# Issuing the overflow path's weight copies from GpSimd's queue instead of ScalarE's

## The chip, the cores and the metric

The kernel runs on one core of a Trainium2 chip. The core has five engines, each with its own instruction stream: TensorE (PE in the profile; its weight loads are listed as PEld), VectorE (DVE), ScalarE (ACT), GpSimd (POOL) and SyncE (SP). A "q" behind an engine's name (SPq) means its sequencer: what it does there is waiting, branching or issuing a DMA, and it isn't counted as busy time. Engines tell each other of finished work by semaphores. The metric is device time in microseconds (us); lower is better.

## The reference, cut to what matters

The program is two transformer blocks on 256 tokens of width 1024. The first ends in a mixture of experts: a router picks one of 4 groups and two of its 8 experts for every token, and each expert is a small gated network (1024 to 2 x 256 to 1024). The reference sorts the 512 assignments by expert and runs every block of 128 slots:

```python
def run_block(args):
    xb, e, wb = args
    a = jax.nn.silu(xb @ w_gate[e]) * (xb @ w_up[e])
    return (a @ w_down[e]) * wb[:, None].astype(xb.dtype)
```

No expert may drop a token, however many it is given. The second block (three kinds of attention and a convolutional feed-forward network) reads the result.

## The kernel before, in words

The program runs mixer, mixture of experts (`moe`, L928) and second block (`block2`, L1294) one after the other. Instructions are written in Python; a scheduler sets the order on each engine, and a framework adds the semaphore waits.

**Experts.** `moe` gives each expert 32 slots and takes 4 experts at a time: 8 batches, loop over `b` at L1204. A batch needs 12 weight pieces of 1 MB (128 x 2048 f32): 8 for gate and up (`egu`), 4 for down (`edn`). For each piece `gateup1` (L1089) or `down` (L1148) does 4 products, which the trace shows as 8 matmuls. Between them come: the gather of tokens (L1072, copied to `xg` on L1074 and L1077), the gate (L1002 to L1004), two transposes (L1113, L1122), a copy of the down product out of PSUM to the tile `eo` (`out`, L1137, on ScalarE), and the scatter (L1131 on TensorE from `eo`, L1132 on VectorE into the residual `xT`).

**Weight loads.** `issue` (L280, its DMA is L284) sends the pieces from SyncE in the order in which they are used, into 23 buffers. The framework gives DMAs from SyncE and ScalarE eight semaphores in turn (DMAHW0 to DMAHW7), and a load waits until the load eight places before it has landed. There are 99 such loads; the last 13 of them stand behind the branch below.

**The two spare paths.** After batch 3 an extra set of 32 slots serves the expert with most tokens (`extra`). After batch 4 (`TURN + 1`), `overflow` (L1240) covers whatever doesn't fit even then. Each engine loads the largest remaining count (L1231) and branches (`tc.If`, L1247). Where the count is above 32, a loop over the batches (L1252) runs all tokens through all experts again, in pieces of 128 x 512 that the inner function `part` copies from HBM (L1255, L1256). Its tiles `wp` share the tag "eo" of pool `tm`, and so the two buffers of the `eo` tiles of L1137.

With these inputs the branch isn't taken: no instruction of L1248 to L1291 is in the trace. What remains of the path is the branch on every engine, with its code in the program, and a few instructions on the other arm of the branch, on which the framework moves the semaphores by as much as the skipped loop would have moved them, so that waits placed after the branch are the same on both ways. The loop's 48 copies a round, dealt over 8 semaphores, would add 6 x 16 = 96 to each.

Of the kernel before, what the change touches and what calls it, by code (L numbers as in the profile page):

```python
# [222 lines left out]
class Prog:  # L223
# [1016 lines left out]
    def overflow(self, tm, pm, psum, hn, W, pos, thr, most):  # L1240


        tc, nc, I = self.tc, self.nc, self.I
        v, a, te = nc.vector, nc.scalar, nc.tensor
        mm = te.matmul
        xT, g2 = self.xT, self.modc[:, 40:48]
        with tc.If(most > CAP, preferred_fallthrough_block=False):  # L1247
            Wo = pm.tile([P, 2, NE], F32, name="Wo")  # L1248
            v.tensor_tensor(out=Wo, in0=pos, in1=thr.unsqueeze(1).to_broadcast([P, 2, NE]), op=OP.is_gt)
            v.tensor_tensor(out=Wo, in0=Wo, in1=W, op=OP.mult)  # L1250
            Wo = Wo.rearrange("p q (b j) -> p q j b", j=4)
            with tc.For_i(0, NE // 4, 1) as b:  # L1252
                for j in range(4):
                    def part(name, i):
                        w = tm.tile([P, 512], F32, name="wp", tag="eo")  # L1255
                        a.dma_start(w, self.I[name].rearrange("b i p (j f) -> b j i p f", j=4)[bass.ds(b, 1), j, i]  # L1256
                                    .rearrange("o p f -> (o p) f"))
                        return w

                    gu = [psum("gu", 2) for _ in range(2)]  # L1260
                    for d in range(KD):
                        w = part("egu", d)
                        o = psum("x", 2)
                        for q in range(2):
                            te.transpose(o[:, q * P:(q + 1) * P], hn[:, q, d * P:(d + 1) * P], self.co("ident"))
                        hT = tm.tile([P, T], F32, name="hT", tag="ga")
                        a.activation(hT, o[:, :T], AF.Identity, scale=self.cols[:, 24 + d:25 + d], bias=self.modc[:, 24 + d:25 + d])
                        for q in range(2):
                            mm(gu[q], hT[:, q * P:(q + 1) * P], w, start=d == 0, stop=d == KD - 1)
                    aT = [tm.tile([P, 2, P], F32, name=n, tag=n, bufs=1) for n in ("aT", "PT")]  # L1270
                    for q in range(2):
                        th = tm.tile([P, 512], F32, name="th", tag="eo")[:, 0:256]
                        ac = tm.tile([P, 256], F32, name="ga", tag="ga")
                        a.activation(th, gu[q][:, 0:256], AF.Tanh, scale=0.5)
                        v.scalar_tensor_tensor(out=ac, in0=th, scalar=1.0, in1=gu[q][:, 0:256], op0=OP.add, op1=OP.mult)
                        v.scalar_tensor_tensor(out=ac, in0=ac, scalar=Wo[:, q, j, bass.ds(b, 1)], in1=gu[q][:, 256:512],
                                               op0=OP.mult, op1=OP.mult)
                        o = psum("x", 2)
                        for k in range(2):
                            te.transpose(o[:, k * P:(k + 1) * P], ac[:, k * P:(k + 1) * P], self.co("ident"))  # L1280
                        a.copy(aT[q], o[:, 0:256].rearrange("p (k s) -> p k s", k=2))
                    for nh in range(2):
                        wd = [part("edn", 2 * nh + k) for k in range(2)]
                        for q in range(2):
                            for i in range(4):
                                d = 4 * nh + i
                                o = psum("c", 2)
                                for k in range(2):
                                    mm(o[:, :P], wd[k][:, i * P:(i + 1) * P], aT[q][:, k], start=k == 0, stop=k == 1)
                                v.scalar_tensor_tensor(out=xT[:, d, q * P:(q + 1) * P], in0=o[:, :P], scalar=g2[:, d:d + 1],  # L1290
                                                       in1=xT[:, d, q * P:(q + 1) * P], op0=OP.mult, op1=OP.add)  # L1291
# [534 lines left out]
```

## Time and profile before

| | us |
|---|---|
| median of 3 runs | 1007.67 (1006.49 to 1008.81) |
| the profiled execution's own time | 1006.2 |
| its span, first to last instruction | 1004.4 |
| TensorE busy in the span | 928.5 |
| batches 0 to 7 of the experts, about | 341 to 553 |
| the branch, by engine | 342 (POOL), 463 (ACT), 467 (PE), 468 (DVE), 486 to 506 (SP) |

The last two lines are positions in the span. The weight loads are read in three ways: the order in which SyncE issues them (the timeline of SP), how long one takes from issue to landing (the DMA list of a stretch with one issue in it), and what the DMA engines move (the windows: "DMA share" 1.0 means that all 16 are busy).

### The profile page before, as it was taken

How to read it: one execution, taken by the hardware profiler on the slowest of the kernel's cores; microseconds unless marked ns; L12 is line 12 of the kernel's file. 1: busy time of each engine (PE TensorE's matmuls, PEld its weight loads, DVE VectorE, ACT ScalarE, POOL GpSimd, SP SyncE). 2: the span in 40 equal slices, each digit the busy share in tenths (PEclk: the TensorE clock that was granted, in tenths of full speed). 3: DMA queues.
4: the chain of work that ended last, by engine and by line, in shares of the span. 5: the costliest groups of instructions: out<-in, count | busy, mean ns of one | idle time of the engine just before them, and what ended most of it. 6: DMA issues, size and time to landing. Idle time of an engine off the chain costs nothing. (4 is left out here: it accounts for less than half of the span.)

```text
span 1004.4 us, 17784 instructions
## 1 busy us (share of the span) xinstructions
PE 928.5 (92%) x6870; PEld 761.9 (76%) x6870; DVE 604.9 (60%) x1463; ACT 473.3 (47%) x1006; POOL 13.0 (1%) x28
## 2 busy tenths in 40 slices
PE   4899899999999899997698999899998999999995
PEld 2678888999999545443232898788898889999994
DVE  2468699664663524223123884787769687676764
ACT  3546866555443122121112765476754565555553
POOL 0000000000000000000000000000001000000001
PEclk9899899999999799998989999999999999999998
DMA  8977367669558599999989654643245344555501
GB/s 358 408 275 283 123 243 264 248 233 421 223 204 355 196 420 416 413 422 418 418 344 421 250 189 149 250 152 137 92 169 189 126 169 168 193 185 174 205 1 43
DMA packets 37387, 249.76 MB, mean 249 GB/s; under 512 B 4272, under 2 KB 5040, under 8 KB 8368
## 3 DMA queue, kind: packets, MB, share of 16 engines
q1 hardware_dynamic: 37008, 248.01, 64.0%
q8 instruction: 56, 0.92, 0.4%
q10 hardware_dynamic: 288, 0.55, 0.2%
q14 instruction: 35, 0.29, 0.1%
HBM read 247.49 MB, written 1.05 MB: 247 GB/s over the span
## 5 line engine op out<-in xcount | busy, mean ns | idle before, releaser
L301 DVE TENSOR_TENSOR wlo<-w,whi 128x512 fp32r<-128x512 f32 (+2 forms) x426 | 287.9, 683 | 152.8 <-ACT whi L300 137.5
L300 ACT CAST whi<-w 128x512 fp32r<-128x512 f32 (+2 forms) x426 | 257.7, 611 | 253.1 <-PE ps_a L317 195.2
L316 PE MATMUL ps_a<-hh,whi 128*128 128x256 f32 x304 | 79.1, 292 | 4.9 <-ACT hh L612 3.1
L317 PE MATMUL ps_a<-hl,whi 128*128 128x256 f32 x304 | 78.5, 289 | 0.0
L1132 DVE SCALAR_TENSOR_TENSOR xT<-ps_c,modc,xT 128x256 f32<-128x256 f32 x72 | 33.1, 483 | 72.7 <-PE ps_c L1131 72.6
L316 PE MATMUL ps_a<-h4h,whi 128*128 128x256 f32 x304 | 76.1, 283 | 0.2 <-ACT h4h L343 0.2
L317 PE MATMUL ps_a<-h4l,whi 128*128 128x256 f32 x304 | 76.1, 283 | 0.0
L1089 PE MATMUL ps_gu<-w,xg 128*32 128x512 f32 x512 | 68.7, 618 | 6.5 <-issue 6.5
L316 PEld LDWEIGHTS ps_a<-hh,whi 128*128 128x128 f32 x304 | 59.4, 196 | 9.1 <-ACT hh L612 3.3
L316 PE MATMUL ps_a<-h2h,whi 128*128 128x256 f32 x248 | 64.2, 289 | 0.5 <-DVE kn L1509 0.5
L317 PE MATMUL ps_a<-h2l,whi 128*128 128x256 f32 x248 | 63.0, 284 | 0.0
L317 PEld LDWEIGHTS ps_a<-hl,whi 128*128 128x128 f32 x304 | 59.6, 196 | 2.0 <-issue 1.2
L316 PEld LDWEIGHTS ps_a<-h4h,whi 128*128 128x128 f32 x304 | 58.1, 192 | 1.2 <-ACT h4h L343 0.6
L317 PEld LDWEIGHTS ps_a<-h4l,whi 128*128 128x128 f32 x304 | 58.2, 192 | 0.3
L1131 PE MATMUL ps_c<-PT,eo 128*128 128x256 f32 (+1 forms) x144 | 41.9, 410 | 13.1 <-ACT eo L1137 12.1
L1131 PEld LDWEIGHTS ps_c<-PT,eo 128*128 128x128 f32 (+1 forms) x144 | 24.3, 192 | 37.3 <-ACT eo L1137 16.4
L1072 PEld LDWEIGHTS ps_x<-Ph,hn 128*128 128x128 f32 x256 | 34.0, 198 | 22.4 <-issue 17.6
L321 PE MATMUL ps_a<-hh,wlo 128*128 128x256 f32 x304 | 49.9, 288 | 0.3 <-DVE wlo L301 0.3
L316 PEld LDWEIGHTS ps_a<-h2h,whi 128*128 128x128 f32 x248 | 47.4, 191 | 2.9 <-issue 1.8
L321 PE MATMUL ps_a<-h4h,wlo 128*128 128x256 f32 x304 | 48.7, 283 | 0.0
L1077 ACT ACTIVATE xg<-ps_x,modc,cols 128x128 f32<-128x128 f32 x32 | 14.6, 457 | 70.4 <-PE ps_x L1072 60.9
L317 PEld LDWEIGHTS ps_a<-h2l,whi 128*128 128x128 f32 x248 | 47.4, 191 | 0.2 <-issue 0.2
(527 smaller groups left out, 1998.5 us busy)
## 6 DMA issues: line engine op xcount, KB each, us to landing
w<-in_egu_dram SPq DMA_DIRECT2D x66, 1024.0 KB, 18.4
w<-in_edn_dram SPq DMA_DIRECT2D x33, 1024.0 KB, 19.8
w<-in_up_dram SPq DMA_DIRECT2D x22, 1024.0 KB, 4.7
w<-in_w2a_dram SPq DMA_DIRECT2D x20, 1024.0 KB, 6.6
w<-in_mod_dram SPq DMA_DIRECT2D x19, 1024.0 KB, 7.0
w<-in_win_og_dram SPq DMA_DIRECT2D x12, 1024.0 KB, 5.9
w<-in_dn_dram SPq DMA_DIRECT2D x11, 1024.0 KB, 4.8
w<-in_br_dram SPq DMA_DIRECT2D x8, 1024.0 KB, 12.5
```

The source lines that it names most:

```text
L300: nc.scalar.copy(hi, src)
L301: nc.vector.tensor_tensor(out=lo, in0=src, in1=hi.bitcast(F32), op=OP.subtract)
L316: mm(out, hi[:, s], ah[:, k], start=first, stop=False)
L317: mm(out, hi[:, s], al[:, k], start=False, stop=False)
L321: mm(out, lo[:, s], ah[:, k], start=False, stop=last)
L1072: mm(o[:, i * P:(i + 1) * P], hn[:, q, d * P:(d + 1) * P], Phs[b][q], start=q == 0, stop=q == 1)
L1077: a.activation(xgs[0][:, i], o[:, i * P:(i + 1) * P], AF.Identity, scale=ac[:, d:d + 1], bias=modc[:, 24 + d:25 + d])
L1089: mm(gu[32 * j:32 * j + 32], xgs[d // 4][:, d % 4, j * CAP:(j + 1) * CAP], w[:, j * 512:(j + 1) * 512], start=d == 0, stop=d == KD - 1)
L1131: mm(o[:, i * T:(i + 1) * T], eo_[:, (d0 + i) * P:(d0 + i + 1) * P], PT, start=True, stop=True)
L1132: v.scalar_tensor_tensor(out=xT[:, d], in0=o[:, i * T:(i + 1) * T], scalar=g2[:, d:d + 1], in1=xT[:, d], op0=OP.mult, op1=OP.add)
```

## The change

One line: the 48 copies a round of the loop are issued by `nc.gpsimd` instead of `a`, which is `nc.scalar`.

```diff
                     def part(name, i):
                         w = tm.tile([P, 512], F32, name="wp", tag="eo")
-                        a.dma_start(w, self.I[name].rearrange("b i p (j f) -> b j i p f", j=4)[bass.ds(b, 1), j, i]
+                        nc.gpsimd.dma_start(w, self.I[name].rearrange("b i p (j f) -> b j i p f", j=4)[bass.ds(b, 1), j, i]
                                     .rearrange("o p f -> (o p) f"))
                         return w
```

DMAs of GpSimd have semaphores of their own in this framework (DMASW0 to DMASW7), so the other arm of the branch changes too. Three places show it; the names in brackets are the semaphores that an instruction, or the sequencer just before it, waits for.

SyncE, from its last load ahead of the branch to the head of the skipped loop; "-" is before, "+" now:

```order
 L284 DMA w<-in_edn_dram 128x2048 [waits DMAHW7_49,PE_49]
 L1247 COMPARE_AND_BRANCH
-L1247 UNCONDITIONAL_BRANCH [waits DMAHW0_49,DMAHW1_49,DMAHW2_49,DMAHW3_49,DMAHW4_49,DMAHW5_49,DMAHW6_49,DMAHW7_49]
+L1247 UNCONDITIONAL_BRANCH
 L1252 COMPARE_AND_BRANCH
```

Before, on the arm that is taken here, SyncE waited for each of the eight semaphores of its own loads in turn and added 96 to it. Now it only jumps.

GpSimd, at the same branch (the 48 copies of the loop body and what stands with them, 96 more rows, follow behind the last one shown):

```order
 L1231 TENSOR_LOAD ci [waits DVE_49]
 L1247 COMPARE_AND_BRANCH
+L1247 ISA [waits DMASW4_49,DMASW5_49,DMASW3_49,DMASW6_49,DMASW2_49,DMASW7_49,DMASW1_49,DMASW0_49]
 L1247 UNCONDITIONAL_BRANCH
 L1252 COMPARE_AND_BRANCH
+L1252 ISA [waits DMASW4_49,DMASW5_49,DMASW3_49,DMASW6_49,DMASW2_49,DMASW7_49,DMASW1_49,DMASW0_49]
 L1252 UNCONDITIONAL_BRANCH
```

The first added row is the counterpart on the arm that is taken: one instruction that adds 96 to all eight DMASW semaphores. What it waits for is a count of zero, because no DMA has been issued on GpSimd before it.

ScalarE, behind the branch, in batch 5 (`aT` and `PT` are the transposed gate and places, `ga` the gate):

```order
 L1002 ACTIVATE ga<-ps_gu 128x256 [waits DVE_49,PE_49,Activation_49]
 L1115 COPY aT<-ps_x 128x256 [waits PE_49,Activation_49]
 L1123 COPY PT<-ps_x 128x256 [waits PE_49,Activation_49]
-L1137 COPY eo<-ps_dn 128x512 [waits DMAHW4_49,DMAHW2_49,DMAHW6_49,DMAHW0_49,PE_49]
-L1137 COPY eo<-ps_dn 128x512 [waits DMAHW3_49,DMAHW5_49,DMAHW1_49,DMAHW7_49,DVE_49,PE_49]
+L1137 COPY eo<-ps_dn 128x512 [waits DMASW4_49,DMASW2_49,DMASW6_49,DMASW0_49,PE_49]
+L1137 COPY eo<-ps_dn 128x512 [waits DMASW3_49,DMASW5_49,DMASW1_49,DMASW7_49,DVE_49,PE_49]
 L1077 ACTIVATE xg_3865<-ps_x,modc,cols 128x128 [waits PE_49,Activation_49] x3
```

The first two `eo` copies behind the branch reuse the buffers of `wp`, so they wait for the loop's copies to have been counted: before on the counts that SyncE raised, now on those that GpSimd raises. The order of the executed instructions is the same on every engine.

## Rows read from the trace of the kernel before

**Rows 1.** The page: the span, and each engine's busy time.
```profile
span 1004.4 us, 17784 instructions
PE 928.5 (92%) x6870; PEld 761.9 (76%) x6870; DVE 604.9 (60%) x1463; ACT 473.3 (47%) x1006; POOL 13.0 (1%) x28
```

**Rows 2.** ACT's waits: us in total, times, longest.
```profile
ACT eo L1137 <- SPq L1247: 13.0, 1, 13.0
```

**Rows 3.** SP's waits, 380 to 620 us, same columns.
```profile
SPq L1247 <- SPq L1247: 20.1, 8, 3.2
```

**Rows 4.** Line L1247: count, ns least/median/most, first and last start.
```profile
L1247 SPq EVENT_SEMAPHORE  x8: 17/17/17, 487.8 to 506.0; - x8
L1247 POOLq COMPARE_BRANCH  x2: 38/42/45, 342.0 to 342.1; - x2
...
L1247 PEldq COMPARE_BRANCH  x2: 95/3117/6139, 467.0 to 467.3; - x2
```

**Rows 5.** Timeline of ACT, 489 to 510 us: start, length, [idle before].
```profile
503.63 0.58 ACT L1137 COPY eo<-ps_dn 128x512 f32<-128x512 f32 x1 [13.01 <-SPq L1247]
```

**Rows 6.** Timeline of PE, 490 to 512 us, same columns.
```profile
492.81 1.16 PE L1072 MATMUL ps_x<-Ph,hn 128*128 128x128 f32 x8
504.27 2.07 PE L1131 MATMUL ps_c<-PT,eo 128*128 128x256 f32 x4 [10.31 <-ACT eo L1137]
...
507.82 1.13 PE L1131 MATMUL ps_c<-PT,eo 128*128 128x256 f32 x4
```

**Rows 7.** Windows: length, busy by engine, granted clock, DMA share, GB/s.
```profile
500.00:504.00 4.00, 0.00 (x0) 0.00 (x0) 0.00 (x0) 0.37 (x1) 0.00 (x0) 0.50 0.77 322
504.00:508.00 4.00, 3.73 (x13) 1.56 (x14) 0.97 (x2) 0.25 (x2) 0.00 (x0) 0.57 0.17 43
508.00:512.00 4.00, 4.00 (x26) 2.31 (x30) 1.91 (x5) 1.01 (x2) 0.00 (x0) 1.00 0.97 389
```

**Rows 8.** Timeline of PE, 524 to 556 us (batches 6 and 7).
```profile
525.81 1.13 PE L1131 MATMUL ps_c<-PT,eo 128*128 128x256 f32 x4
...
527.86 1.13 PE L1131 MATMUL ps_c<-PT,eo 128*128 128x256 f32 x4
...
532.73 6.22 PE L1089 MATMUL ps_gu<-w,xg 128*32 128x512 f32 x56
...
541.38 3.51 PE L1148 MATMUL ps_dn<-w,aT 128*32 128x512 f32 x16 [0.30 <-ACT aT L1115]
```

**Rows 9.** Timeline of SP, 425 to 479 us: loads ahead of the branch.
```profile
430.68 17.74 SPq L284 DMA_DIRECT2D w<-in_egu_dram  x8
...
460.50 17.80 SPq L284 DMA_DIRECT2D w<-in_egu_dram  x8
```

**Rows 10.** DMA issued at 485.4 us, last before the branch: KB, us to landing.
```profile
w<-in_edn_dram SPq DMA_DIRECT2D x1, 1024.0 KB, 20.5
```

**Rows 11.** DMA issued at 506.6 us, first behind the branch.
```profile
w<-in_edn_dram SPq DMA_DIRECT2D x1, 1024.0 KB, 4.8
```

**Rows 12.** DMA issued at 511.4 us, ninth behind it.
```profile
w<-in_egu_dram SPq DMA_DIRECT2D x1, 1024.0 KB, 21.3
```

**Rows 13.** DMA issued at 516.5 us, eleventh behind it.
```profile
w<-in_edn_dram SPq DMA_DIRECT2D x1, 1024.0 KB, 21.1
```

**Rows 14.** DMA issued at 525.3 us: the second block's first weights.
```profile
w<-in_w2a_dram SPq DMA_DIRECT2D x1, 1024.0 KB, 19.8
```

**Rows 15.** Timeline of ACT, 545 to 561 us: first use of those weights.
```profile
553.53 2.16 ACT L300 CAST whi<-w 128x512 fp32r<-128x512 f32 x4
```

**Rows 16.** Timeline of POOL, 300 to 560 us: its first instruction there.
```profile
519.66 0.31 POOL L1470 MEMSET hv<- 128x256 f32 x1 [426.97 <-PE ps_gu L1089]
```

**Rows 17.** Windows of the experts' end, columns as in rows 7.
```profile
532.00:548.00 16.00, 13.36 (x91) 4.15 (x92) 3.30 (x9) 2.55 (x6) 0.00 (x0) 0.89 1.02 422
541.50:545.00 3.50, 3.39 (x16) 0.46 (x13) 0.00 (x0) 0.11 (x2) 0.00 (x0) 0.51 1.01 421
548.00:556.00 8.00, 6.00 (x41) 2.93 (x40) 6.57 (x16) 6.65 (x16) 0.00 (x0) 1.00 1.01 419
```

## Prediction, made before the changed kernel ran

> **What bounds the kernel now.** I read the page's first lines, then the waits at the branch, then the stretch around it on each engine, and last the weight loads.
>
> TensorE is busy for 928.5 of 1004.4 us [rows 1], so an idle time of TensorE is where something is to be had. ScalarE's waits show one that belongs to the line of the branch: an `eo` copy waits 13.0 us, once, for SyncE's sequencer on L1247 [rows 2]. SyncE's own waits name the cause: eight on L1247, 20.1 us together [rows 3]. They stand before eight semaphore instructions of 17 ns each, from 487.8 to 506.0 us [rows 4]: SyncE lets each of its eight outstanding loads land before it adds to that load's semaphore. The last load ahead of the branch was issued at 485.4 and took 20.5 us, to 505.9 [rows 10]; the last addition is at 506.0. So nothing is in flight behind it.
>
> That costs twice. First, the `eo` copy starts at 503.63 behind 13.01 us of waiting [rows 5]; TensorE, done with its matmuls at 492.81 + 1.16 = 493.97, has nothing to do until the scatter that reads `eo`, at 504.27: 10.31 us [rows 6]. It then runs at the lower of its two levels (granted clock 0.50, 0.57, then 1.00 [rows 7], that is 1.2 and 2.4 GHz): from the first scatter to the second are 507.82 − 504.27 = 3.55 us, against 527.86 − 525.81 = 2.05 for the same pair in the next batch [rows 8], 1.5 us more. Second, the transfers stop: 322, 43 and 389 GB/s in three windows of 4 us [rows 7], where 420 or so is the full rate [rows 17]. Missing are (98 + 377 + 31) x 4 / 420 = 4.8 us of transfer.
>
> **The change part by part.**
>
> *SyncE's hold goes.* The eight waits and additions leave SyncE's stream on the arm that runs. Behind the last load ahead of the branch it jumps and goes on issuing, each load when the one eight places before has landed.
>
> *ScalarE's wait changes its source.* The first two `eo` copies now wait for GpSimd's addition. GpSimd passes the branch at 342.0 [rows 4]. The copy is wanted at 503.63 − 13.01 = 490.6, so the addition has 148 us to spare; for one of the two buffers this is a wait for a count long reached.
>
> *GpSimd gets one instruction.* The trace of before has none like it. The nearest rows are SyncE's additions, 17 ns, and the longest instruction of any engine on this line, 6139 ns of TensorE's branch [rows 4]. Both ends vanish in those 148 us; and GpSimd's own next work is at 519.66, after 426.97 us of idling [rows 16]. I take 0. It cannot gain. Nothing else queues behind it, since the loop's 48 copies are on the arm not taken.
>
> *TensorE's branch* stays: the 6139 ns are its own and the change moves none of its instructions.
>
> *What is late next.* If nothing else waited, TensorE would get back 10.31 + 1.5 = 11.8 us. But it then meets the loads earlier, and those can't all come earlier by as much. One load takes 1048.6 KB / 422 GB/s = 2.485 us of the transfer rate [rows 17]; twelve loads, the two groups of eight issues with the four between them, give (460.50 − 430.68) / 12 = 2.485 too [rows 9].
>
> Behind the branch stand 13 loads. The first was issued at 506.6 and landed at 511.4 [rows 11]; the ninth was issued at 511.4 and landed at 532.7 [rows 12]. That ninth piece feeds the last eight of the 56 gate matmuls that run from 532.73 for 6.22 us [rows 8], so it is wanted at 532.73 + 48/56 x 6.22 = 538.06, or 5.3 us after it landed. The eleventh, landed at 516.5 + 21.1 = 537.6 [rows 13], feeds the second half of the 16 down matmuls from 541.38 for 3.51 us [rows 8], at about 543.1: 5.5 us to spare. Without the hold the ninth would land nine loads after 505.9: at 2.485 each 528.3, 4.4 us earlier than now. At the pace after the gap (eight pieces in 21.3 us, 2.66 each) it would be 505.9 + 2.5 + 8 x 2.66 = 529.7, 3.0 earlier. So the last batch can come 5.3 + 3.0 = 8.3 to 5.3 + 4.4 = 9.7 us earlier before it waits for that piece; the eleventh gives 5.5 + 3.0 to 4.4 = 8.5 to 9.9, so the ninth decides. I take 9.2, nearer to the undisturbed pace, since the crowding behind the gap came from the gap. Of the 11.8 us, 2.6 then turn up as short waits of TensorE for loads in the last batch.
>
> The second block takes its first weights at 553.53 [rows 15]; they landed at 525.3 + 19.8 = 545.1 [rows 14], 8.4 us ahead. They too come some 4.4 earlier, and use by 9.2, so 3.6 us remain. I count nothing there.
>
> A half-clock stretch stands in the same place already: 541.5 to 545 at 0.51 [rows 17], worth 3.39 x 0.49 = 1.7 us. With short waits ahead of it, it may go or come twice: ±1.7.
>
> *Sum.* −9.2 − 0 + 0 = −9.2 us. Against the profiled execution's own 1006.2 (its span of 1004.4 and 1.8 around it) this is 997.0. The median shown is 1.5 higher, 1007.67, so **998.5 us**. The forecast's own range goes from −11.8 (the loads keep pace after all) to −6.6 (−8.3 and another half-clock stretch): 995.9 to 1001.1, and the runs of before spread by about 1.2 either way, so 995 to 1002.
>
> **The rivals.**
>
> *Only the lost transfers come back.* In the stretch from 532 on the DMA share is 1.01 to 1.02 [rows 17], and SyncE's issues come at the rate of the transfers [rows 9]. If the experts' end were paced by loads alone, with no slack, the gain would be the missing transfer time, 4.4 to 4.8 us: 1003.1 with 4.6. Against it stand the 5.3 and 5.5 us that the ninth and eleventh pieces lie ready: before, the last batch is still late by TensorE's idling, not by loads. It would be true if an earlier piece than these had far less to spare.
>
> *No change.* The `eo` copy waits just as long, for GpSimd, and SyncE is held by something else: 1007.7. For this GpSimd's addition would have to come 148 us late. Nothing on GpSimd could hold it: it idles from before the branch to 519.66 [rows 16]. The Trainium skill, page "DMA: Bandwidth & Descriptors", section "Issuing engines are not separate DMA queues", speaks for this case too: transfers started by ScalarE, SyncE or GpSimd run on the same 16 DMA engines, and another issuing engine saves only the usually small time of starting them. By it, with no copy executed here, the time would stay at 1007.7. The trace disagrees for this kernel, since what is saved isn't the start of a copy but SyncE's 20.1 us of waiting for counts [rows 3].
>
> *Slower: TensorE waits for one piece at a time and falls to half clock until the second block.* Now 13.36 us of TensorE's work in 532 to 548 and 6.00 in 548 to 556 [rows 17], less the 6.22 of the 56 gate matmuls [rows 8], are 13.1 us that follow the last gate pieces. If TensorE, come 9 us earlier, had to wait for each piece there and ran this whole stretch at half clock, they would take 13.1 more, of which 1.7 are paid already: +11.4 against −9.2, 1009.9. It makes the change a loss once more than 9.2 + 1.7 = 10.9 of those 13.1 us run at the lower level. Against it: after a whole 10.31 us without work the clock was back at 1.00 by the window from 508 [rows 7], and the one low stretch of the last batch ends within 3.5 us or little more [rows 17]. The page "TensorE: Matmul & The Clock Gate" of the Trainium skill, section "HAM oscillation — how this bites in real kernels", describes this case: bursts of matmuls with a wait for a transfer between them, each burst starting at the low clock. No stretch of the rows here shows such a row of bursts.
>
> **How the numbers follow.** A difference of 0.2%, 2.0 us, is about what a measurement of this kernel can tell from no change. The forecast, wait gone and the last batch paced by its loads, gets 0.77; only the transfers back 0.12; no change 0.06; slower 0.05. The first two are faster by more than 0.2%: 0.89; within it 0.06; slower 0.05. The range leaves out the last two and about 0.05 at the edges: 995.0 to 1003.2.
>
> **What would show it.** In the changed kernel's trace: no wait of SyncE on L1247, and loads landing every 2.5 us through 500 to 512; ScalarE's first `eo` copy of batch 5 near 491 without a wait of 10 us; the scatter behind it at full clock; GpSimd's new instruction near 342 and nothing waiting for it; in the last batch waits of TensorE for weight pieces, 2 to 3 us in all, the ninth landing near 528; the second block's first weight use near 544. If the `eo` copy's wait has only changed its releaser, or TensorE waits 5 us or more for pieces, or the clock stays near 0.5 past the last batch, the prediction is wrong at that step.

## The result, and the profile after

The changed kernel takes 997.11 us (median of 4 runs, 995.0 to 998.63) against 1007.08 for the kernel before on the same chip: a ratio of 0.9897, with a 95% interval of 0.9877 to 0.9916. Two more timings of the same kernel beside later experiments gave 0.9917 (0.9895 to 0.9939) and 0.9913 (0.9895 to 0.993). So it is 8 to 10 us faster; the forecast was 998.5. The profiled execution of after is its fastest, 995.0. In it TensorE is already 1.3 us ahead of the one of before at the matmuls ahead of the first scatter (491.51 against 492.81), and the loads 0.7 at the last one ahead of the branch (issued at 484.70 against 485.4); in what follows TensorE's 1.3 is taken off where the two are compared.

The page, as in [rows 1]:

```profile
span 993.3 us, 17788 instructions
PE 927.3 (93%) x6870; PEld 760.9 (77%) x6870; DVE 605.6 (61%) x1463; ACT 473.6 (48%) x1006; POOL 13.0 (1%) x28
```

The span is 11.1 us shorter and TensorE's busy time 1.2: what went is waiting.

Line L1247 by engine, as in [rows 4] (count, ns least/median/most, first and last start):

```profile
L1247 POOLq EVENT_SEMAPHORE  x4: 17/42/43, 341.1 to 341.3; - x4
...
L1247 PEldq COMPARE_BRANCH  x2: 91/3046/6000, 466.0 to 466.3; - x2
...
L1247 SPq COMPARE_BRANCH  x2: 38/48/57, 485.1 to 485.2; - x2
L1247 POOLq INC_SWDGE_SEM  x1: 158/158/158, 341.4 to 341.4; - x1
```

SyncE's eight semaphore instructions are gone, and no wait of SyncE on this line is left. GpSimd has five in their place, not the one of the section on the change and of the prediction: four semaphore instructions of at most 43 ns from 341.1 on, and the addition, 158 ns at 341.4. TensorE's 6 us at the branch are still there.

ScalarE at the first `eo` copy behind the branch, as in [rows 5], and TensorE around it, as in [rows 6] (start, length, [idle before]):

```profile
490.79 0.59 ACT L1137 COPY eo<-ps_dn 128x512 f32<-128x512 f32 x1 [1.46 <-PE ps_dn L1148]
```

```profile
491.51 1.16 PE L1072 MATMUL ps_x<-Ph,hn 128*128 128x128 f32 x8
492.50 1.03 PE L1131 MATMUL ps_c<-PT,eo 128*128 128x256 f32 x4
...
494.46 1.13 PE L1131 MATMUL ps_c<-PT,eo 128*128 128x256 f32 x4
```

The copy waits 1.46 us for its product instead of 13.01 for SyncE. TensorE runs on, at full clock: from the first scatter to the second are 494.46 − 492.50 = 1.96 us, where before there were 3.55. The second scatter stands at 494.46 instead of 507.82, 13.4 us earlier; less the 1.3, TensorE has gained 12.1 here.

The windows, as in [rows 7] and [rows 17] (busy by engine, then granted clock, DMA share, GB/s):

```profile
500.00:504.00 4.00, 3.99 (x37) 1.59 (x40) 0.83 (x2) 0.56 (x2) 0.00 (x0) 1.00 1.02 424
504.00:508.00 4.00, 3.58 (x33) 1.67 (x23) 1.23 (x4) 0.84 (x2) 0.81 (x3) 1.00 1.01 418
508.00:512.00 4.00, 4.00 (x35) 1.71 (x34) 1.07 (x4) 1.33 (x3) 0.00 (x0) 1.00 1.02 424
...
530.00:533.50 3.50, 3.11 (x16) 1.26 (x20) 0.15 (x1) 0.75 (x2) 0.00 (x0) 0.52 1.02 424
```

The transfers don't stop: 424, 418, 424 GB/s in place of 322, 43, 389. One half-clock stretch (0.52) lies in the last batch, as before.

TensorE in the last batch, as in [rows 8], and two loads, as in [rows 10, 12]: the last ahead of the branch, issued at 484.70, and the ninth behind it, issued at 507.70 (KB, us to landing):

```profile
519.38 4.50 PE L1089 MATMUL ps_gu<-w,xg 128*32 128x512 f32 x40
525.08 1.07 PE L1089 MATMUL ps_gu<-w,xg 128*32 128x512 f32 x8 [1.21 <-DMA w<-in_egu_dram]
527.73 1.07 PE L1089 MATMUL ps_gu<-w,xg 128*32 128x512 f32 x8 [1.58 <-DMA w<-in_egu_dram]
...
531.48 2.82 PE L1148 MATMUL ps_dn<-w,aT 128*32 128x512 f32 x16
```

```profile
w<-in_edn_dram SPq DMA_DIRECT2D x1, 1024.0 KB, 20.5
...
w<-in_egu_dram SPq DMA_DIRECT2D x1, 1024.0 KB, 20.0
```

The 56 gate matmuls that ran through before are now 40, 8 and 8, with waits of 1.21 and 1.58 us for pieces between them. The ninth piece lands at 507.70 + 20.0 = 527.7, and its matmuls start at 527.73: what lay ready for 5.3 us before is now used at once. From the last load ahead of the branch, landed at 484.70 + 20.5 = 505.2, these are 22.5 us, nine times 2.50; before they were 26.8. The down matmuls follow at 531.48 instead of 541.38: 9.9 us earlier, 8.6 without the 1.3.

ScalarE's first use of the second block's weights, as in [rows 15]:

```profile
542.70 2.16 ACT L300 CAST whi<-w 128x512 fp32r<-128x512 f32 x4
```

553.53 − 542.70 = 10.8 us earlier, 9.5 without the 1.3. From 12.1 us gained at the scatter, 9.5 come through (10.1 if only the 0.7 us of the loads, which now set the pace here, are taken off).

### The profile page after: what moved, and what is told of

Same layout as the page of the kernel before. It is cut to its first block, busy times and chain, and to the rows that moved or that the text cites. A ratio compares the mean times of both kernels' runs of the same rounds, so it can differ in the third digit from the quotient of the medians.

```text
span 993.3 us, 17788 instructions
## 1 busy us (share of the span) xinstructions
PE 927.3 (93%) x6870; PEld 760.9 (77%) x6870; DVE 605.6 (61%) x1463; ACT 473.6 (48%) x1006; POOL 13.0 (1%) x28
## 4 chain that ended last, share of the span: by engine, by line
PE 78%; DMA 13%; DVE 4%; ACT 3%; issue 1%; SPq 0%; ACTq 0%; DVEq 0%
PE ps_a L316 16%; PE ps_a L317 16%; PE ps_a L321 16%; DMA w<-in_egu_dram 8%; PE ps_acc L1784 6%; DMA w<-in_edn_dram 4%; PE ps_gu L1089 3%; PE ps_x L1072 2%; PE ps_md L502 2%; PE ps_a L338 2%; PE ps_a L340 2%; PE ps_a L339 2%; PE ps_dn L1148 1%; PE ps_c L1131 1%; DVE wlo L301 1%
## 5 line engine op out<-in xcount | busy, mean ns | idle before, releaser
L1077 ACT ACTIVATE xg<-ps_x,modc,cols 128x128 f32<-128x128 f32 x32 | 14.6, 458 | 70.0 <-PE ps_x L1072 60.5
L1089 PEld LDWEIGHTS ps_gu<-w,xg 128*32 128x32 f32 x512 | 15.0, 111 | 41.0 <-issue 32.2
```

Source lines behind the costliest of these rows:

```text
L1089: mm(gu[32 * j:32 * j + 32], xgs[d // 4][:, d % 4, j * CAP:(j + 1) * CAP], w[:, j * 512:(j + 1) * 512], start=d == 0, stop=d == KD - 1)
```

## Experiments

Each was timed in five rounds against the kernel before on the same chip; ratios are to that kernel, with 95% intervals. The theory is that of the prediction: two costs at the branch (TensorE's idling through the `eo` wait, and the gap in the loads through SyncE's hold), of which the last batch feels the later one.

**The issuing engine, or the semaphores?** The copies are issued by SyncE instead of ScalarE, everything else as before.

```diff
-                        a.dma_start(w, self.I[name].rearrange("b i p (j f) -> b j i p f", j=4)[bass.ds(b, 1), j, i]
+                        nc.sync.dma_start(w, self.I[name].rearrange("b i p (j f) -> b j i p f", j=4)[bass.ds(b, 1), j, i]
```

> The kernel before, with the loop's copies issued from SyncE's queue instead of ScalarE's. Theory (what counts is the group of semaphores that the skipped copies would have counted on, which SyncE and ScalarE share, not the engine that issues them): SyncE still waits for its eight loads at the branch, about 20 us together, the first eo copy of batch 5 still waits some 13 us, and the time is that of before, 1007 us, ratio 1.000 within 0.002. Rival (what counts is that ScalarE no longer has the copies in its stream): the eo copy runs at once, TensorE's 10.3 us of idling go, and the time is near 997, ratio 0.990.

Measured: 1.0009 (0.9994 to 1.0024). The waits of ScalarE and of SyncE's queue, in us, times, longest, beside [rows 2, 3]:

```profile
ACT eo L1137 <- SPq L1247: 13.2, 1, 13.2
```

```profile
SPq L1247 <- SPq L1247: 20.2, 8, 3.4
```

Both are as they were. So it is worth nothing that ScalarE no longer issues the copies. What the change is worth comes with GpSimd's own semaphores, which count none of the weight loads: with them the eight waits and the 13 us are gone from the trace of after.

**The hold alone.** Copies on ScalarE's queue as before, but into a tile that no `eo` copy shares. It is smaller, and the loop, which doesn't run here, is fitted to it.

```diff
-                    def part(name, i):
-                        w = tm.tile([P, 512], F32, name="wp", tag="eo")
+                    def part(name, i, w=None, n=256):
+                        w = pm.tile([P, KD, CAP], F32, name="xs").rearrange("p k c -> p (k c)") if w is None else w
...
```

> The kernel before, with the copies still on ScalarE's queue but into a tile that no eo copy shares (it is smaller, so the loop, which does not run here, would take half of each piece). SyncE's hold of about 20 us at the branch stays; ScalarE's wait for it goes. Theory (two costs, and a slack between them): TensorE comes back 11 to 12 us earlier in batch 5, but the last batch's pieces land when they did before, the ninth behind the branch near 532.7, where 5.2 us were spare; so the gain stops at about 5.2 us: 1002 us, ratio 0.995, and TensorE waits 6 to 7 us for pieces in the last batch. Rival A (the eo wait is the whole price): 997, ratio 0.990. Rival B (only the transfers' gap counts): no change, 1007.

Measured: 0.9956 (0.994 to 0.9972), 1001.86 us. SyncE still waits eight times, and the transfers still stop (windows, columns as above):

```profile
SPq L1247 <- SPq L1247: 19.8, 8, 2.5
```

```profile
500.00:504.00 4.00, 4.00 (x44) 1.04 (x32) 0.41 (x1) 0.46 (x1) 0.00 (x0) 1.00 0.60 248
504.00:508.00 4.00, 3.58 (x28) 2.18 (x28) 1.57 (x4) 1.59 (x4) 0.81 (x3) 1.00 0.35 104
...
528.00:532.00 4.00, 2.90 (x16) 0.40 (x16) 0.00 (x0) 0.00 (x0) 0.00 (x0) 0.50 1.01 422
```

The `eo` copy waits only for its product, so TensorE is in time at the scatter. It then waits for one piece after the other, 6.0 us in all, at half clock from the third wait on (0.50 in the last window above):

```profile
488.97 0.59 ACT L1137 COPY eo<-ps_dn 128x512 f32<-128x512 f32 x1 [1.46 <-PE ps_dn L1148]
```

```profile
520.20 1.06 PE L1089 MATMUL ps_gu<-w,xg 128*32 128x512 f32 x8 [0.72 <-DMA w<-in_egu_dram]
522.68 1.06 PE L1089 MATMUL ps_gu<-w,xg 128*32 128x512 f32 x8 [1.41 <-DMA w<-in_egu_dram]
526.52 1.94 PE L1089 MATMUL ps_gu<-w,xg 128*32 128x512 f32 x8 [2.77 <-DMA w<-in_egu_dram]
529.00 1.94 PE L1089 MATMUL ps_gu<-w,xg 128*32 128x512 f32 x8 [0.55 <-DMA w<-in_egu_dram]
531.49 1.93 PE L1089 MATMUL ps_gu<-w,xg 128*32 128x512 f32 x8 [0.55 <-DMA w<-in_egu_dram]
```

So the gain, 4.4 us (2.8 to 6.0), ends about where the 5.3 us of spare time end, as expected: neither the whole (rival A) nor nothing (rival B).

**TensorE's lateness alone, first try.** The changed kernel, with a copy on GpSimd meant to hold its addition back until 503.

```diff
+        late = pm.tile([P, KD, CAP], F32, name="xs")
+        self.nc.gpsimd.tensor_copy(late[:, 0, 0:1], self.ahead[-2][:, 0:1])
         with tc.If(most > CAP, preferred_fallthrough_block=False):
```

> The changed kernel, with one small copy on GpSimd ahead of the branch that reads the last but one weight piece issued there, so that GpSimd adds to its semaphores only when that piece has landed, near 503.5 us. SyncE is not held. Theory: the eo copy waits some 13 us for GpSimd, TensorE idles 10 us as before, the pieces land some 5 us earlier than before and lie ready for 10 us in the last batch: 1007 us, ratio 1.000 within 0.002. Rival B (only the transfers' gap counts): 1002 to 1003, ratio 0.995. Rival A gives 1007 too.

Measured: 0.9915 (0.9892 to 0.9939), the changed kernel's time. The edit didn't do what it was for. GpSimd's line L1247 and its copy, L1242, in the trace:

```profile
L1247 POOLq INC_SWDGE_SEM  x1: 158/158/158, 344.2 to 344.2; - x1
...
L1242 POOL COPY xs<-w x1: 185/185/185, 506.2 to 506.2; 128x1 f32<-128x1 f32 x1
```

The scheduler had put the copy behind the branch, so the addition still came at 344.2. The run says nothing of the theory. Nor does it hold GpSimd back: its next own work stood at 506.3 in after, too.

**The same, by work on TensorE.** The changed kernel, with the first two products of a scatter of batch 5 made many times over.

```diff
-                        mm(o[:, i * T:(i + 1) * T], eo_[:, (d0 + i) * P:(d0 + i + 1) * P], PT, start=True, stop=True)
+                        [mm(o[:, i * T:(i + 1) * T], eo_[:, (d0 + i) * P:(d0 + i + 1) * P], PT, start=True, stop=True) for _ in range(1 + (0 if d0 else more))]
...
-                down(aT, PT, b == NB - 1)
+                down(aT, PT, b == NB - 1, 25 * (b == TURN + 2))
```

> The changed kernel with 50 more matmuls in the first scatter of batch 5: each of its first two products is made 26 times instead of once (the same result over itself), 50 x 0.24 = 12 us of TensorE's work where the kernel before idled 10.3 us. SyncE is not held, the loads land 5 us earlier than before. Theory (the last batch ends at the later of loads and TensorE): TensorE's lateness of before is back, pieces lie ready for 9 to 10 us, the waits of the last batch (3.2 us) go, and the time is the changed kernel's plus 12.0 - 3.2 = 8.8: 1006 us, ratio 0.9985 within 0.002. Rival B (only the transfers' gap counts): 1002, ratio 0.995.

Measured: 1.0058 (1.0037 to 1.008), slower than before. The expectation had counted a product as one matmul; it is two, so the edit added 100 matmuls of 0.216 us, 21.6 us and not 12. From the changed kernel beside it (0.9913) the step is 0.0145, 14.6 us, so 7.0 us are swallowed; the two intervals together leave nearly 3 us either way. With 6 in place of 25 it added 24 matmuls, 5.2 us:

> As the run with 50 more matmuls, with 12 more: 2.9 us of TensorE's work added to the changed kernel in batch 5. Theory: it is swallowed by the 3.2 us that TensorE waits for pieces in the last batch: the changed kernel's time within 0.5 us, ratio 0.990 to 0.991. Rival (TensorE bounds the last batches, its work always counts): 2.9 us more, 1000, ratio 0.993 to 0.994.

Measured: 0.99 (0.988 to 0.992), beside 0.9913 (0.9895 to 0.993) for the changed kernel in the same rounds:

> The changed kernel beside the two runs with added matmuls: 997 to 998 us, ratio 0.990 to 0.992.

The added work doesn't show. In full it would have made 0.9913 + 0.0052 = 0.9965, above the interval. In the trace of this run the added work stands in two groups of matmuls in batch 5, and the last batch's 56 gate matmuls run through again:

```profile
493.72 3.62 PE L1131 MATMUL ps_c<-PT,eo 128*128 128x256 f32 x16
...
499.12 3.72 PE L1131 MATMUL ps_c<-PT,eo 128*128 128x256 f32 x16
...
525.17 6.21 PE L1089 MATMUL ps_gu<-w,xg 128*32 128x512 f32 x56
```

The waits for pieces are gone; the added work has taken their place. How much of the 5.2 us is swallowed, 3 or all, this interval of 2 us either way doesn't tell. With 14 in place of 25 comes the amount that was wanted, 56 matmuls:

> The changed kernel with 56 more matmuls of 0.216 us in the first scatter of batch 5 (each product is two matmuls, so the runs before this one had added 100 and 24, not 50 and 12): 12.1 us of TensorE's work where the kernel before lost 11.8. SyncE is not held and the loads land 5 us earlier than before. Theory: of the 12.1 us the last batch's waits and half-clock stretch swallow 4.5, and the time is the changed kernel's plus 7.6: 1005.5 us, ratio 0.9985 within 0.002; pieces lie ready for 8 us or more. Rival B (only the transfers' gap counts): 1002, ratio 0.995.

Measured: 0.9984 (0.9968 to 1.0), 1005.21 us, as the theory had it and clear of rival B's 0.995. The added work in batch 5, windows, TensorE in the last batch, and the ninth load behind the branch, issued at 510.51:

```profile
494.97 7.07 PE L1131 MATMUL ps_c<-PT,eo 128*128 128x256 f32 x32
...
504.69 7.17 PE L1131 MATMUL ps_c<-PT,eo 128*128 128x256 f32 x32
```

```profile
500.00:504.00 4.00, 4.00 (x30) 2.14 (x32) 0.92 (x2) 0.59 (x1) 0.00 (x0) 1.00 1.00 416
504.00:508.00 4.00, 4.00 (x23) 2.95 (x16) 0.00 (x0) 0.46 (x1) 0.00 (x0) 1.00 1.01 422
```

```profile
533.91 6.22 PE L1089 MATMUL ps_gu<-w,xg 128*32 128x512 f32 x56
542.50 1.92 PE L1148 MATMUL ps_dn<-w,aT 128*32 128x512 f32 x16 [0.30 <-ACT aT L1115]
```

```profile
w<-in_egu_dram SPq DMA_DIRECT2D x1, 1024.0 KB, 19.8
```

The transfers never stop, and the ninth piece lands at 530.3; its matmuls, the last eight of the 56, start near 533.91 + 48/56 x 6.22 = 539.2. It lies ready for nearly 9 us, and the time is all but that of before. An unbroken stream of loads is worth next to nothing while TensorE is late, at most 0.3% by the interval. The 1.6 us that are left are as much as the down matmuls save by running at full clock here, 1.92 us against 3.51; that they come from there was not tested.

**Without the path.** The branch, the loop and the reading of the count are left out, and with them TensorE's 6 us at the branch.

```diff
-                    with tc.issue_after(last):
-                        most = nc.values_load(ci[0:1, 1:2], min_val=0, max_val=T)
-                    self.overflow(tm, pm, psum, hn, W, pos, thr, most)
+                    pass
```

> The overflow path is left out whole (its branch, its loop and the read of its count); it does not run with these inputs. No hold, no eo wait, and none of TensorE's 6 us stop at the branch either. Theory (the last batch is now paced by loads that come one every 2.49 us and have been at the full transfer rate since batch 1): TensorE only waits about 6 us longer for the last pieces, and the time is that of the changed kernel, 997 us, ratio 0.990 within 0.002. Rival (TensorE's idle time is lost time wherever it lies): 6 us less, 991, ratio 0.984.

Measured: 0.9899 (0.9881 to 0.9918), 997.34 us, the changed kernel's time. TensorE, which was there sooner, waits more often:

```profile
521.18 1.07 PE L1089 MATMUL ps_gu<-w,xg 128*32 128x512 f32 x8 [2.47 <-DMA w<-in_egu_dram]
523.68 1.94 PE L1089 MATMUL ps_gu<-w,xg 128*32 128x512 f32 x8 [1.44 <-DMA w<-in_egu_dram]
526.17 1.50 PE L1089 MATMUL ps_gu<-w,xg 128*32 128x512 f32 x8 [0.55 <-DMA w<-in_egu_dram]
528.65 1.06 PE L1089 MATMUL ps_gu<-w,xg 128*32 128x512 f32 x8 [0.98 <-DMA w<-in_egu_dram]
```

So the changed kernel pays nothing that can be told any more for the path that it doesn't run.

**Two loads fewer.** The last batch uses its first piece three times, after the change and before it.

```diff
+                w = kept["w"] = kept["w"] if (b, d) in ((7, 1), (7, 2)) else self.weights()
...
+                    self.order += [c for i, c in enumerate(self.chunks(NB - 1)) if i not in (1, 2)]
```

> The changed kernel without the second and third weight piece of the last batch: the first one is used in their place (so the last batch's experts compute something else), and two loads of 1 MB fewer stand behind the branch. Theory (loads pace the last batch, and TensorE has about 2.8 us of waits and 1.6 us of half clock left there): 3 to 4.5 us less than the changed kernel, 993, ratio 0.986. Rival (something else sets the last batch's end): as the changed kernel, 997, ratio 0.990.

> The kernel before without the same two loads, the first piece of the last batch used three times. Theory (before, TensorE's idling made the last batch late and every piece lay ready for 5 us): no gain, 1007 us, ratio 1.000 within 0.002. Rival (the loads paced the last batch before, too): 4 to 5 us less, 1002.5, ratio 0.9955.

Measured: after the change 0.985 (0.983 to 0.987), 992.74 us, 4.7 to 6.7 thousandths below the three ratios of the changed kernel; before it 0.9988 (0.9973 to 1.0003), no gain that can be told. The same 2 MB count in one kernel and not in the other. In the trace of the second TensorE idles at the scatter as ever:

```profile
505.72 2.08 PE L1131 MATMUL ps_c<-PT,eo 128*128 128x256 f32 x4 [10.59 <-ACT eo L1137]
```

A last repetition of the changed kernel stood beside the first three experiments:

> The changed kernel once more, beside the others on one chip. Theory: 997 us, ratio 0.990; the two parts (no eo wait, no hold of SyncE) together give about 10 us where each alone gives 5 and 0.

It gave the 0.9917 above. The four cells stand together:

| | TensorE late in batch 5 | TensorE in time |
|---|---|---|
| loads held | 1 (before) | 0.9956 |
| loads not held | 0.9984 (late by added work) | 0.9897 to 0.9917 (after) |

## Why the prediction was right

- *SyncE's hold goes, and ScalarE's wait has a new source that is always early.* Shown in the trace of after; the run with SyncE as issuer shows that taking the copies off ScalarE alone doesn't do it. The price of GpSimd's instruction, bounded by 17 and 6139 ns and taken as nothing, is 158 ns behind four short semaphore instructions, 149 us before it is needed.
- *TensorE gets back 11.8 us at the scatter.* It got 12.1.
- *The last batch can use only 8.3 to 9.7 of them.* This was the step that made the number. The ninth piece was to come nine loads of 2.49 to 2.66 us behind the last one ahead of the branch; it came after nine of 2.50, so at the undisturbed end, as was chosen. The waits were to be 2.6 us, and are 1.21 + 1.58 = 2.8. The gain to the second block's first weights is 9.5 (forecast 9.2), to the down matmuls 8.6. The eleventh piece, which the prediction had 0.2 us behind the ninth in spare time, is nearly as tight: in after it landed at 512.66 + 20.0 = 532.7, 0.5 us before its matmuls at 533.2. The run with the hold alone and the one with 56 more matmuls show both limits separately.
- *Half clock, ±1.7.* In the profiled execution of after there is one stretch at 0.52 in place of one at 0.51; the 16 down matmuls take 2.82 us, before 3.51, so the term came out near nothing. In those of the two later timings the stretch came twice (below), as the term allowed.
- *Only the lost transfers come back (1003.1).* Wrong: with the transfers alone restored, the time is 0.9984, and restored transfers are worth something only once TensorE is in time.
- *No change.* By the page "DMA: Bandwidth & Descriptors" of the Trainium skill (section "Issuing engines are not separate DMA queues"), starting transfers from several engines saves only the time of starting them. Here 8 to 10 us were saved though no copy was started before or after, so what was saved is something else. The run with SyncE as issuer bears that out from the other side: moving the copies between engines that share the semaphores of the loads gave 1.0009.
- *Slower, by half clock between pieces.* Its mechanism exists, though the rows of before showed no such bursts: with the loads held and TensorE in time, three bursts of eight matmuls take 1.94 us instead of 1.06, one behind the other. The first two of them cost nothing, as they end 0.55 us before the next piece, which comes 2.48 us after the last (526.52, 529.00, 531.49). What the rival had wrong is how long it lasts. Its price, 11.4 us, took all 13.1 us of work behind the last gate piece to run at half clock; in this run the clock is at full again from 540 on, and the 16 down matmuls take no longer than the 3.51 us of before:

```profile
536.11 3.17 PE L1148 MATMUL ps_dn<-w,aT 128*32 128x512 f32 x16
```

```profile
536.00:540.00 4.00, 3.19 (x17) 0.60 (x16) 0.00 (x0) 1.01 (x3) 0.00 (x0) 0.67 1.01 422
540.00:544.00 4.00, 3.95 (x24) 1.67 (x24) 2.85 (x7) 1.58 (x4) 0.00 (x0) 1.00 1.01 420
```

What stays open is how the 2 us between the three timings of the changed kernel (0.9897 against 0.9913 and 0.9917) come about, which their intervals don't exclude to be chance. In the profiled executions of the two later timings, gate bursts in the last batch ran at half clock, in the first none did, and the half-clock stretch came twice. A burst and the two stretches, from the second timing (0.9917):

```profile
526.72 1.93 PE L1089 MATMUL ps_gu<-w,xg 128*32 128x512 f32 x8 [1.42 <-DMA w<-in_egu_dram]
```

```profile
526.80:530.20 3.40, 2.85 (x16) 0.31 (x16) 0.00 (x0) 0.00 (x0) 0.00 (x0) 0.50 1.01 422
...
533.60:537.00 3.40, 2.84 (x16) 0.37 (x8) 0.00 (x0) 0.46 (x1) 0.00 (x0) 0.50 1.01 422
```

But little of the difference between these executions lies there. The last load ahead of the branch, issued at 485.52, and the first use of the second block's weights:

```profile
w<-in_edn_dram SPq DMA_DIRECT2D x1, 1024.0 KB, 21.2
```

```profile
544.80 2.16 ACT L300 CAST whi<-w 128x512 fp32r<-128x512 f32 x4
```

The load landed at 506.8, 1.6 us later than in the first execution (505.2), before any gate burst of the last batch; at the second block's weights the two are 2.1 us apart (544.8 against 542.7). That leaves some 0.5 us to the half clock; a further 0.7 of the 2.8 us between the spans (996.1 against 993.3) arises behind. In the third execution it is much the same up to there: 506.7 and 544.7.

## What to carry to other kernels

A path that is never taken can cost time by the bookkeeping on its other arm: look for waits that belong to the line of the branch itself, and ask with which DMAs the skipped ones share their semaphores. When a stop is removed, compute how long the next inputs lay ready behind it; the gain ends at that spare time plus what the inputs themselves come earlier. Here two costs lay on top of each other, and undoing the one alone gave 0.4%, the other at most 0.3%, both together 0.8 to 1.0%.

## What the runs showed of the hardware that was not expected

- Bursts of matmuls at half clock cost nothing where they ended before the next piece landed: in the run with the hold alone, 1.94 us of work per 2.48 us, with the granted clock at 0.50. The last burst of that row, with no piece to wait for behind it, took 1.93 us instead of 1.06.
- GpSimd's addition to all eight of its semaphores is one instruction of 158 ns behind four semaphore instructions of at most 43 ns, where SyncE needed eight of 17 ns with a wait before each, 20.1 us in all.
- TensorE's 5.9 to 6.1 us at the branch, in each of the twelve traces that have it, cost nothing that can be told once the loads set the pace: 0.9899 without it, 0.9897 to 0.9917 with it.
